# Pre norm's weights on the first token tile by features, and eight identity products ahead of the work

## Chip, cores and metric

The kernel runs on one core of one Trainium2 chip. The metric is the device time of one execution in microseconds; several executions of each kernel are timed and their median is taken. Beside the timed runs there is one profiled execution, whose own time stands beside the span of its trace. TensorE (PE) multiplies matrices, VectorE (DVE) and ScalarE (ACT) work elementwise, GpSimd (POOL) does small scalar steps here, and SyncE (SP) mostly issues DMA transfers.

## The reference, cut to what matters

One decoder layer over 1024 tokens of 1024 features, all float32:

```
h = x * rsqrt(mean(x*x) + 1e-6) * pre_norm_g        # per token; pre_norm_g has one weight per feature
z = h @ w_in                                        # 1024 x 6160
... branch A: gated spatial unit; branch B: gated linear attention ...
y = x + rmsnorm(concat(A, B) @ w_out, post_norm_g)
```

Only the first line and the start of the second are touched by the change.

## The kernel before

The tokens are cut into eight tiles of 128 and the features into eight groups of 128. All matmuls need the feature index on the partitions, so each token tile is normalised with tokens on the partitions and then transposed by TensorE against an identity matrix. A product in nearly full float32 precision is made of three float32r products: every operand is kept as a rounded high part and the remainder as a low part (`split`, lines 106 to 108: ScalarE copies to the rounded type, VectorE subtracts), and `mm3` (lines 110 to 115) issues high x high (L113), high x low (L114) and low x high (L115). The normalised and transposed tokens are the tiles `hTh` and `hTl`, "hT" in the trace.

`load(t)` (lines 246 to 250) fetches token tile t on SP's DMA queue, tile 0 in two halves. `prep(t)` (lines 252 to 276) makes hT of it: ScalarE squares and sums (L259 for tile 0, L263 for the others), GpSimd adds epsilon and raises to the power -0.5 (`rsqrt`, L98 or L100, then L103), VectorE multiplies each half of the tile by this number per token and by the weights, which lie in the tile `gain`, repeated over all 128 partitions (L267), TensorE transposes four groups of 128 features into one PSUM bank (L273), and `split` writes the high and low part of the half (L107, L108).

`block_a` (lines 127 to 147) fetches a block of `w_in` of 512 columns in four granules of two feature groups each. A granule is a raw tile of 512 KB, loaded in two DMAs of 256 KB, and its split into high and low parts ("gr" in the trace). There are three raw buffers. The first block's first two granules (`early=2`) are issued on ScalarE's DMA queue and the other two on SP's. The argument `before` is called ahead of every granule; here it issues the load of token tile 1 ahead of granule 2.

`first_block((t,))` (lines 204 to 207) multiplies token tile t by the eight feature groups of the first block, 24 products into one PSUM bank (`proj_tok`, lines 173 to 181). In the loop of lines 292 to 300 the products of tile t stand between the preparation of the tiles behind it.

The order of an engine's instructions is set when the program is built: a scheduler simulates the program and lets each engine take, of what is ready in its simulation, the instruction that stands first in the source. On the chip every engine then runs its list in that order and waits at an instruction whose operands are not there.

The source order before, around the change (lines 278 to 286):

```
load(0, 2)
gain = pre.tile([P, D], F32, name="gain", bufs=1)
nc.sync.dma_start(gain, row_bc(pre_g, D))
prep(0)
blk = block_a(((C_BV, DV), (C_BG, DV)), lambda k2: load(1) if k2 == 2 else None, fine=True, early=2)
load(2)
```

`row_bc` reads the 4 KB of weights once for each of the 128 partitions, so that this transfer writes 512 KB.

Of the kernel before, what the change touches and what calls it, by code (L numbers as in the profile page):

```python
# [8 lines left out]
F32 = mybir.dt.float32  # L9
F32R = mybir.dt.float32r  # L10
U8 = mybir.dt.uint8
AF = mybir.ActivationFunctionType
ALU = mybir.AluOpType
PSUM = bass.MemoryType.PSUM

P = 128
S = 1024
D = 1024
NT = S // P
KT = D // P  # L20
H = 4
DK = 128
DV = 256
# [5 lines left out]
C_Q, C_K, C_BV, C_BG, C_LR = 3072, 3584, 4096, 5120, 6144  # L29
# [4 lines left out]
def hybrid_layer(  # L34
# [16 lines left out]
    nc = tc.nc  # L51
    x, out = x[0], out[0]
    pre_g, w_in, w_a2, b_a2 = pre_g[0], w_in[0], w_a2[0], b_a2[0]
# [3 lines left out]
    def row_bc(v, n):  # L57
        return v.rearrange("(o n) -> o n", o=1).to_broadcast([P, n])
# [10 lines left out]
    def bank():  # L69
        return psum.tile([P, 512], F32, tag="ps", name="ps")  # L70
# [18 lines left out]
    ident = const.tile([P, P], F32, name="ident")  # L89
    make_identity(nc, ident)  # L90

    LINE = 32
# [3 lines left out]
    def rsqrt(dst, mean, more=None):  # L96
        if more is None:
            nc.gpsimd.tensor_scalar(out=dst, in0=mean, scalar1=EPS, scalar2=None, op0=ALU.add)  # L98
        else:
            nc.gpsimd.tensor_scalar(  # L100
                out=dst, in0=mean, scalar1=EPS, scalar2=more, op0=ALU.add, op1=ALU.add
            )
        nc.gpsimd.tensor_tensor(out=dst, in0=dst, in1=neghalf[:, : dst.shape[-1]], op=ALU.pow)  # L103


    def split(hi, lo, src, eng=None):
        nc.scalar.copy(out=hi, in_=src)  # L107
        return (eng or nc.vector).tensor_tensor(out=lo, in0=src, in1=hi.bitcast(F32), op=ALU.subtract)  # L108
# [10 lines left out]
    def granule(shape):  # L119

        g = wts.tile([P, 2] + shape, F32R, tag="gr", name="gr", bufs=4)
        return g[:, 0], g[:, 1]

    def raw_tile(shape):
        return wts.tile([P] + shape, F32, tag="raw", name="raw", bufs=3)

    def block_a(cols, before=lambda k2: None, fine=False, early=0):

        got = []
        for k2 in range(KT // 2):  # L130
            before(k2)
            raw = raw_tile([2, W])
            c = 0
            for c0, n in cols:
                (nc.scalar if k2 < early else nc.sync).dma_start(
                    raw[:, :, c : c + n],
                    w_in[k2 * 256 : (k2 + 1) * 256, c0 : c0 + n].rearrange("(k p) c -> p k c", p=P),
                )
                c += n
            hi, lo = granule([2, W])  # L140
            if fine:
                for j in range(2):
                    split(hi[:, j], lo[:, j], raw[:, j])
            else:
                split(hi, lo, raw)
            got += [(hi[:, j], lo[:, j]) for j in range(2)]
        return got

    def block_b(cols):
# [15 lines left out]
    hTh, hTl = (  # L165
        [hp.tile([P, 4, S], F32R, tag="q", name="hT", bufs=4) for _ in range(2)] for _ in range(2)
    )
# [36 lines left out]
    def first_block(ts):  # L204
        for t, p in zip(ts, proj_tok(ts, blk)):
            nc.scalar.copy(out=v0[:, t], in_=p[:, 0:DV])
            evac_gate(sg0[:, t], p[:, DV:], bg0)
# [29 lines left out]
    def next_unit(after):  # L237
        if units:
            sums = wout_sums(*units.pop(0))
            with tc.issue_after(after.ins):  # L240
                sums()

    with tc.tile_pool(name="pre", bufs=2) as pre:
        xts = {}

        def load(t, n=1):
            xts[t] = pre.tile([P, D], F32, tag="xt", name="xt", bufs=3)
            for i in range(n):
                c = slice(i * D // n, (i + 1) * D // n)
                nc.sync.dma_start(xts[t][:, c], x[t * P : (t + 1) * P, c])  # L250

        def prep(t):
            xt = xts.pop(t)
            h = pre.tile([P, D], F32, tag="h", name="h", bufs=2)
            ss = pre.tile([P, LINE], F32, tag="ss", name="ss", bufs=3)
            halves = [slice(j * W, (j + 1) * W) for j in range(2)]
            if t == 0:
                for j, c in enumerate(halves):
                    nc.scalar.activation(  # L259
                        out=h[:, c], in_=xt[:, c], func=AF.Square, scale=D ** -0.5, accum_out=ss[:, j : j + 1]  # L260
                    )
            else:
                nc.scalar.activation(out=h, in_=xt, func=AF.Square, scale=D ** -0.5, accum_out=ss[:, 0:1])  # L263
            rstd = ss[:, 0:1]
            rsqrt(rstd, rstd, ss[:, 1:2] if t == 0 else None)
            for j, c in enumerate(halves):
                nc.vector.scalar_tensor_tensor(  # L267
                    out=h[:, c], in0=xt[:, c], scalar=rstd, in1=gain[:, c], op0=ALU.mult, op1=ALU.mult
                )
                pt = bank()  # L270
                for k in range(4):
                    kk = 4 * j + k
                    nc.tensor.transpose(pt[:, k * P : (k + 1) * P], h[:, kk * P : (kk + 1) * P], ident)  # L273
                ts = slice(t * P, (t + 1) * P)
                last = split(hTh[j][:, :, ts], hTl[j][:, :, ts], pt.rearrange("p (k c) -> p k c", k=4))
            return last

        load(0, 2)

        gain = pre.tile([P, D], F32, name="gain", bufs=1)  # L280
        nc.sync.dma_start(gain, row_bc(pre_g, D))
        prep(0)
        blk = block_a(
            ((C_BV, DV), (C_BG, DV)), lambda k2: load(1) if k2 == 2 else None, fine=True, early=2
        )
        load(2)
        bg0 = const.tile([P, DV], F32, tag="bg", name="bg0")
        nc.gpsimd.dma_start(bg0, row_bc(bn_g[0:DV], DV))
        nc.sync.dma_start(
            lr_raw, w_in[:, C_LR : C_LR + RANK].rearrange("(k p) c -> p k c", p=P)  # L290
        )
        for t in range(NT - 2):
            first_block((t,))
            if t + 3 < NT:
                load(t + 3)
            if t == 0:
                prep(1)
            last = prep(t + 2)
            if t >= 1:
                next_unit(last)  # L300
# [3 lines left out]
    with tc.tile_pool(name="gla", bufs=1) as gp:  # L304
# [3 lines left out]
            out=causal, in_=causal, pattern=[[1, P]], base=0, channel_multiplier=-1,  # L308
# [11 lines left out]
        for i in range(4):  # L320
# [4 lines left out]
            out=w2[32:64], in0=w2_raw[32:64], in1=w2[32:64].bitcast(F32), op=ALU.subtract  # L325
# [8 lines left out]
        for r, w in enumerate(w_lr):  # L334
            nc.gpsimd.memset(w.bitcast(F32), 0.0)
            src = lr_raw[:, 4 * r : 4 * r + 4]
            for i in (0, 1, 3):
                nc.scalar.copy(out=w[:, :, 32 * i : 32 * i + RANK], in_=src)
            nc.gpsimd.tensor_tensor(
                out=w[:, :, 64 : 64 + RANK], in0=src, in1=w[:, :, 0:RANK].bitcast(F32), op=ALU.subtract  # L340
# [4 lines left out]
        for hf in range(2):  # L345
            first_block((NT - 2 + hf,))
            pl = bank()
            c = slice(hf * 512, (hf + 1) * 512)
            for k in range(KT):
                for i, part in enumerate(hT(k, c)):  # L350
                    nc.tensor.matmul(
                        pl, w_lr[k // 4][:, k % 4], part,
                        start=(k == 0 and i == 0), stop=(k == KT - 1 and i == 1),
# [3 lines left out]
                out=lrT[96:128, c], in0=pl[96:128], in1=lrT[96:128, c].bitcast(F32), op=ALU.subtract  # L357
# [201 lines left out]
    with tc.tile_pool(name="sgu", bufs=1) as sp_:  # L559
# [38 lines left out]
        def third_sum_h(k):  # L598
# [8 lines left out]
            out=wsr, in_=wsr, pattern=[[0, G], [-1, P]], base=0, channel_multiplier=1,  # L607
# [11 lines left out]
        for i in range(2):  # L619
            if i == 1:  # L620
                blk = block_a(((C_V + 512, 512),))
            for n, t in enumerate(range(NT) if i == 0 else (4, 5, 6, 7, 0, 1, 2, 3)):
# [5 lines left out]
                if (i, n) == (0, 4):  # L628
                    for r in range(2):
                        pt = bank()  # L630
                        for g in range(4):
                            nc.tensor.transpose(pt[:, g * P : (g + 1) * P], wsr[:, 4 * r + g], ident)
                        nc.scalar.copy(
                            out=wsT[:, 4 * r : 4 * r + 4], in_=pt.rearrange("p (g c) -> p g c", g=4)
# [5 lines left out]
                if (i, n) == (1, 2):  # L640
                    ones = wide()[:, 0:P]
                    nc.vector.memset(ones, 1.0)
                    for r in range(2):
                        pt = bank()
                        nc.tensor.matmul(
                            pt, ones, wsT[:, 4 * r : 4 * r + 4].rearrange("p g t -> p (g t)"),
                            start=True, stop=True,
                        )
                        for g in range(4 * r, 4 * r + 4):
                            nc.vector.scalar_tensor_tensor(  # L650
                                out=q[:, g], in0=pt[:, (g % 4) * P : (g % 4 + 1) * P],
                                scalar=gb[:, 1, g : g + 1], in1=q[:, g], op0=ALU.mult, op1=ALU.add,
# [300 lines left out]
```

## Time and profile before

| | us |
|---|---|
| median of 3 runs | 778.92 |
| lowest, highest run | 777.01, 778.99 |
| the profiled execution's own time | 777.7 |
| span of its trace (first to last instruction) | 776.0 |
| TensorE busy in it | 748.8 |

The times in the trace count from the start of the span. "Busy" counts instructions that run, not what an engine waits for; matmuls are pipelined and overlap, so the step from one to the next is shorter than a matmul's duration. Behind a row, square brackets hold the idle time of the engine in front of it and what ended it. The line numbers are those of the kernel printed above.

### The profile page before, as it was taken

The numbers are of one execution on the slowest core, as the hardware profiler recorded it, in microseconds if no ns is written. First come the engines' busy times: TensorE is split into PE (matmuls) and PEld (weight loads), VectorE is DVE, ScalarE is ACT, GpSimd is POOL, SyncE is SP. The second block draws the span as 40 slices with busy tenths as digits, with TensorE's granted clock in tenths as the row PEclk, the third lists the DMA queues.
The fourth block names the chain that finished last, engine by engine and source line by source line (L and its number), as shares of the span: only waits on it lengthen the run. The fifth ranks groups of instructions, "written<-read, shape, count | busy, mean of one in ns | idle before, by whom it ended". The sixth has DMA issues, their size and how long they took to land.

```text
span 776.0 us, 10096 instructions
## 1 busy us (share of the span) xinstructions
PE 748.8 (97%) x3676; PEld 620.9 (80%) x3676; DVE 498.2 (64%) x862; ACT 389.8 (50%) x680; POOL 128.8 (17%) x167
## 2 busy tenths in 40 slices
PE   4999999999999999999999999999999999999996
PEld 3887788787888778888878888888888778888885
DVE  4756599746576575653897388656555497534665
ACT  5546567646273735443442227665665652434431
POOL 2333243512222222322100000000000000000043
PEclk9999999999999999999999999999999999999999
DMA  9636510343712562243220022112112595346157
GB/s 311 214 110 205 162 55 2 109 162 109 224 55 102 167 200 82 82 163 109 82 82 1 0 55 58 53 54 55 55 54 66 189 372 216 109 162 245 55 217 271
DMA packets 79938, 98.39 MB, mean 127 GB/s; under 512 B 5584, under 2 KB 62928, under 8 KB 79888
## 3 DMA queue, kind: packets, MB, share of 16 engines
q1 hardware_dynamic: 76224, 89.21, 34.9%
q0 software_dynamic: 2000, 6.43, 2.7%
q10 hardware_dynamic: 1664, 2.10, 0.8%
q8 instruction: 29, 0.48, 0.2%
q14 instruction: 21, 0.17, 0.1%
HBM read 72.56 MB, written 25.17 MB: 126 GB/s over the span
## 4 chain that ended last, share of the span: by engine, by line
PE 72%; DVE 9%; DMA 7%; ACT 6%; issue 3%; SPq 1%; POOL 1%; DVEq 0%; POOLq 0%; ACTq 0%
PE ps L113 23%; PE ps L115 23%; PE ps L114 23%; DMA wb<-in_w_out_dram 3%; DMA wo_d<-wb 2%; PE ps L672 2%; DMA xt<-in_x_dram 1%; DVE wb L224 1%; DVE wb L108 1%; DVE gr L108 1%; SPq L221 1%; POOL f L394 1%; DMA a<-mix_d 1%; DVE og L490 1%; PE ps L497 1%
## 5 line engine op out<-in xcount | busy, mean ns | idle before, releaser
L113 PE MATMUL ps<-gr,hT 128*128 128x512 f32 x384 | 152.0, 398 | 1.6 <-ACT gr L107 1.1
L115 PE MATMUL ps<-gr,hT 128*128 128x512 f32 x384 | 149.7, 391 | 0.0
L114 PE MATMUL ps<-gr,hT 128*128 128x512 f32 x384 | 149.6, 392 | 0.0
L108 DVE TENSOR_TENSOR gr<-raw,gr 128x1024 fp32r<-128x1024 f32 (+1 forms) x97 | 91.1, 960 | 25.2 <-ACT gr L107 24.4
L113 PE MATMUL ps<-hT,gr 128*128 128x512 f32 x256 | 100.3, 394 | 0.7 <-ACT u L745 0.7
L114 PE MATMUL ps<-hT,gr 128*128 128x512 f32 x256 | 100.0, 391 | 0.0
L115 PE MATMUL ps<-hT,gr 128*128 128x512 f32 x256 | 99.1, 394 | 0.2 <-DVE gr L108 0.2
L107 ACT CAST gr<-raw 128x1024 fp32r<-128x1024 f32 (+1 forms) x97 | 79.0, 837 | 29.6 <-PE ps L115 16.3
L113 PE MATMUL ps<-gr,ah 128*128 128x512 f32 x216 | 84.1, 390 | 2.4 <-ACT ah L107 2.4
L113 PEld LDWEIGHTS ps<-gr,hT 128*128 128x128 f32 x384 | 72.5, 189 | 16.6 <-ACT gr L107 1.5
L115 PEld LDWEIGHTS ps<-gr,hT 128*128 128x128 f32 x384 | 72.4, 189 | 14.7 <-DVE hT L108 0.2
L114 PE MATMUL ps<-gr,ah 128*128 128x512 f32 x216 | 84.0, 389 | 0.0
L114 PEld LDWEIGHTS ps<-gr,hT 128*128 128x128 f32 x384 | 72.5, 189 | 13.7
L115 PE MATMUL ps<-gr,al 128*128 128x512 f32 x216 | 82.9, 389 | 0.0
L224 DVE TENSOR_TENSOR wb<-wb 128x256 f32<-128x256 f32 x64 | 28.7, 448 | 44.4 <-DMA wb<-in_w_out_dram 43.7
L115 PEld LDWEIGHTS ps<-hT,gr 128*128 128x128 f32 x256 | 48.1, 188 | 10.8 <-DVE gr L108 0.9
L113 PEld LDWEIGHTS ps<-hT,gr 128*128 128x128 f32 x256 | 48.1, 188 | 10.3 <-ACT u L745 1.2
L114 PEld LDWEIGHTS ps<-hT,gr 128*128 128x128 f32 x256 | 48.1, 188 | 9.6
L113 PEld LDWEIGHTS ps<-gr,ah 128*128 128x128 f32 x216 | 40.6, 188 | 11.2 <-ACT ah L107 2.8
L107 ACT CAST ah<-a 128x512 fp32r<-128x512 f32 x38 | 23.5, 623 | 49.8 <-PE ps L114 42.7
L114 PEld LDWEIGHTS ps<-gr,ah 128*128 128x128 f32 x216 | 40.6, 188 | 8.4
L115 PEld LDWEIGHTS ps<-gr,al 128*128 128x128 f32 x216 | 40.6, 188 | 8.3
(224 smaller groups left out, 1315.0 us busy)
## 6 DMA issues: line engine op xcount, KB each, us to landing
raw<-in_w_in_dram SPq DMA_DIRECT2D x76, 256.0 KB, 3.2
gr<-wo_d SPq DMA_DIRECT2D x16, 1024.0 KB, 4.8
wb<-in_w_out_dram SPq DMA_DIRECT2D x64, 128.0 KB, 2.6
wo_d<-wh SPq DMA_DIRECT2D x16, 512.0 KB, 2.8
wo_d<-wb SPq DMA_DIRECT2D x16, 512.0 KB, 2.9
raw<-in_w_out_dram SPq DMA_DIRECT2D x12, 512.0 KB, 4.0
mix_d<-mixB POOLq DMA_DIRECT2D x8, 512.0 KB, 3.1
raw<-in_w_in_dram SPq DMA_DIRECT2D x8, 512.0 KB, 3.8
```

The source lines that it names most:

```text
L107: nc.scalar.copy(out=hi, in_=src)
L108: return (eng or nc.vector).tensor_tensor(out=lo, in0=src, in1=hi.bitcast(F32), op=ALU.subtract)
L113: nc.tensor.matmul(ps, a[0], b[0], start=start, stop=False, **how)
L114: nc.tensor.matmul(ps, a[0], b[1], start=False, stop=False, **how)
L115: nc.tensor.matmul(ps, a[1], b[0], start=False, stop=stop, **how)
L221: nc.sync.dma_start(b[:, i], w_out[(row + j) * P : (row + j + 1) * P, c : c + 256])
L224: sub = lambda out, a, c: nc.vector.tensor_tensor(out=out, in0=a, in1=c, op=ALU.subtract)
L394: nc.gpsimd.tensor_tensor(out=f, in0=b[:, :, CH - 1 : CH].to_broadcast([P, 8, CH]), in1=b, op=ALU.subtract)
L490: nc.vector.tensor_scalar_mul(og[:, i], og[:, i], oss[:, i : i + 1])
L497: nc.tensor.transpose(ptv[:, k, i], og[:, i, k * P : (k + 1) * P], ident)
L672: nc.tensor.matmul(pt[:, c], part[:, c], wsT[:, g], start=True, stop=True)
```

## The change

For token tile 0 alone, the weights are no longer multiplied in before the transposition. VectorE multiplies the tile by the number per token only (a tensor by one scalar per partition), TensorE transposes, and the weights come in behind that: features then lie on the partitions, so a weight is one scalar per partition. ScalarE copies each group of 128 features with that scalar as its scale, and VectorE makes the low part in one instruction (product minus the high part). Each of the two engines issues four instructions of 128 columns per half where it issued one of 512.

For this the weights are needed as a column per feature group. They are loaded as 8 rows of 128 on ScalarE's DMA queue (4 KB), transposed by TensorE once and copied by VectorE to `gain_col`. The repeated tile `gain`, which tiles 1 to 7 go on using, is loaded later: ahead of granule 3, behind the loads of token tile 1 and of granule 2 on SP's queue.

In front of `prep(0)` eight products of the identity matrix with itself are issued, into a PSUM bank that nothing reads.

```diff
@@ prep(t) @@
             for j, c in enumerate(halves):
-                nc.vector.scalar_tensor_tensor(
-                    out=h[:, c], in0=xt[:, c], scalar=rstd, in1=gain[:, c], op0=ALU.mult, op1=ALU.mult
-                )
+                if t == 0:
+                    nc.vector.tensor_scalar_mul(h[:, c], xt[:, c], rstd)
+                else:
+                    nc.vector.scalar_tensor_tensor(
+                        out=h[:, c], in0=xt[:, c], scalar=rstd, in1=gain[:, c], op0=ALU.mult, op1=ALU.mult
+                    )
                 pt = bank()
                 for k in range(4):
                     kk = 4 * j + k
                     nc.tensor.transpose(pt[:, k * P : (k + 1) * P], h[:, kk * P : (kk + 1) * P], ident)
-                ts = slice(t * P, (t + 1) * P)
-                last = split(hTh[j][:, :, ts], hTl[j][:, :, ts], pt.rearrange("p (k c) -> p k c", k=4))
+                if t > 0:
+                    last = split(hTh[j][:, :, ts], hTl[j][:, :, ts], pt.rearrange("p (k c) -> p k c", k=4))
+                    continue
+                for k in range(4):
+                    g, src = gain_col[:, 4 * j + k : 4 * j + k + 1], pt[:, k * P : (k + 1) * P]
+                    nc.scalar.activation(out=hTh[j][:, k, ts], in_=src, func=AF.Copy, scale=g)
+                    last = nc.vector.scalar_tensor_tensor(
+                        out=hTl[j][:, k, ts], in0=src, scalar=g, in1=hTh[j][:, k, ts].bitcast(F32),
+                        op0=ALU.mult, op1=ALU.subtract,
+                    )
             return last
 
         load(0, 2)
 
+        g_rows = pre.tile([KT, P], F32, name="g_rows", bufs=1)
+        nc.scalar.dma_start(g_rows, pre_g.rearrange("(k p) -> k p", p=P))
+        gain_col = pre.tile([P, LINE], F32, name="gain_col", bufs=1)
         gain = pre.tile([P, D], F32, name="gain", bufs=1)
-        nc.sync.dma_start(gain, row_bc(pre_g, D))
+        pt = bank()
+        nc.tensor.transpose(pt[:, 0:KT], g_rows, ident[0:KT, 0:KT])
+        nc.vector.tensor_copy(gain_col[:, 0:KT], pt[:, 0:KT])
+
+        idle = bank()
+        for _ in range(8):
+            nc.tensor.matmul(idle[:, 0:P], ident, ident, start=True, stop=True)
         prep(0)
+
+        def more(k2):
+            if k2 == 2:
+                load(1)
+            if k2 == 3:
+                nc.sync.dma_start(gain, row_bc(pre_g, D))
+
         blk = block_a(
-            ((C_BV, DV), (C_BG, DV)), lambda k2: load(1) if k2 == 2 else None, fine=True, early=2
+            ((C_BV, DV), (C_BG, DV)), more, fine=True, early=2
         )
```

## Rows read from the trace of the kernel before

**Rows 1.** The page's busy time, share of the span and instructions of each engine.

```profile
PE 748.8 (97%) x3676; PEld 620.9 (80%) x3676; DVE 498.2 (64%) x862; ACT 389.8 (50%) x680; POOL 128.8 (17%) x167
```

**Rows 2.** Timeline of TensorE, 10 to 21 us: start, duration, engine, line, what.

```profile
10.72 1.97 PE L273 MATMUL ps<-ident,h 128*128 128x128 f32 x8 [10.72 <-DVE h L267]
...
13.21 0.79 PE L113 MATMUL ps<-gr,hT 128*128 128x512 f32 x1 [0.52 <-ACT hT L107]
...
16.36 1.08 PE L273 MATMUL ps<-ident,h 128*128 128x128 f32 x8
...
17.20 0.49 PE L114 MATMUL ps<-gr,hT 128*128 128x512 f32 x1
...
20.07 1.03 PE L273 MATMUL ps<-ident,h 128*128 128x128 f32 x8
```

**Rows 3.** Chain of waits, 0 to 32 us: start, us to the next link, what.

```profile
14.43 0.43 PE ps L115
...
17.68 0.23 PE ps L115
```

**Rows 4.** Timeline of POOL, VectorE (DVE) and ScalarE (ACT), 0 to 16 us.

```profile
2.21 0.31 POOL masks.py:199 TENSOR_SCALAR_AFFINE_SELECT ident<-ident 128x128 f32<-128x128 f32 x1
...
5.56 0.63 ACT L259 ACTIVATE h<-xt 128x512 f32<-128x512 f32 x1 [0.95 <-DMA xt<-in_x_dram]
...
6.77 0.57 POOL L103 TENSOR_TENSOR ss<-ss,neghalf 128x1 f32<-128x1 f32 x1
...
7.00 1.29 DVE L108 TENSOR_TENSOR gr<-raw,gr 128x512 fp32r<-128x512 f32 x2 [6.04 <-ACT gr L107]
...
9.91 1.42 DVE L267 SCALAR_TENSOR_TENSOR h<-xt,ss,gain 128x512 f32<-128x512 f32 x2 [1.62 <-DMA gain<-in_pre_norm_g_dram]
...
11.53 1.06 ACT L263 ACTIVATE h<-xt 128x1024 f32<-128x1024 f32 x1 [4.05 <-DMA xt<-in_x_dram]
...
12.59 0.57 ACT L107 CAST hT<-ps 128x512 fp32r<-128x512 f32 x1
...
13.80 1.41 DVE L267 SCALAR_TENSOR_TENSOR h<-xt,ss,gain 128x512 f32<-128x512 f32 x2
```

**Rows 5.** Same timeline, the queues of SyncE (SPq) and ScalarE (ACTq): DMA issues.

```profile
0.79 1.50 ACTq L135 DMA_DIRECT2D raw<-in_w_in_dram  x3
...
1.71 0.42 SPq L281 DMA_DIRECT2D gain<-in_pre_norm_g_dram  x1
...
3.89 0.37 ACTq L135 DMA_DIRECT2D raw<-in_w_in_dram  x1
...
6.68 0.88 SPq L250 DMA_DIRECT2D xt<-in_x_dram  x1
```

**Rows 6.** DMA issues in windows about 1.71, 3.89, 6.68 us: KB, us to landing.

```profile
gain<-in_pre_norm_g_dram SPq DMA_DIRECT2D x1, 512.0 KB, 8.1
...
raw<-in_w_in_dram ACTq DMA_DIRECT2D x1, 256.0 KB, 8.8
...
xt<-in_x_dram SPq DMA_DIRECT2D x1, 512.0 KB, 7.9
```

**Rows 7.** What the DMA engines moved, 0 to 30 us in 40 slices.

```profile
GB/s 0 0 120 212 238 380 373 320 67 272 393 384 407 376 374 414 414 312 322 371 377 418 423 358 407 365 346 346 343 386 375 284 322 328 369 224 268 399 87 0
```

**Rows 8.** Groups by line, shapes apart: count | busy us, mean ns | idle before.

```profile
L490 DVE TENSOR_SCALAR og<-og,oss 128x256 f32<-128x256 f32 x32 | 13.8, 469 | 2.5 <-POOL oss L103 2.4
...
L206 ACT COPY mixB<-ps 128x256 f32<-128x256 f32 x8 | 3.0, 371 | 12.6 <-PE ps L115 12.6
...
L107 ACT CAST hT<-ps 128x512 fp32r<-128x512 f32 x16 | 8.8, 599 | 0.8 <-PE ps L273 0.8
...
L375 ACT ACTIVATE f<-ps,ba 128x512 f32<-128x512 f32 x8 | 5.5, 690 | 6.8 <-PE ps L438 6.7
...
L650 DVE SCALAR_TENSOR_TENSOR q<-ps,gb,q 128x128 f32<-128x128 f32 x8 | 2.1, 340 | 0.0
```

**Rows 9.** Timeline of TensorE, 456.5 to 459.5 us.

```profile
456.82 1.95 PE L672 MATMUL ps<-wsT,vn 128*128 128x128 f32 x16
```

More of the change, by code (lines that the diff above doesn't have):

```diff
@@ L255, in prep @@
             ss = pre.tile([P, LINE], F32, tag="ss", name="ss", bufs=3)
+            ts = slice(t * P, (t + 1) * P)
             halves = [slice(j * W, (j + 1) * W) for j in range(2)]
```

## The prediction

> **What bounds the kernel now.** I read the page's busy shares first: TensorE is busy 97% of the span [rows 1], so the time follows from when its work begins and how little it stands afterwards. The timeline of TensorE comes next [rows 2]. Nothing runs on it until 10.72 us; then come eight transposes of token tile 0, and at 13.21 the first product of the input projection. The steps are the second thing to see: the chain of waits spaces products by 0.43 us at 14.43 and by 0.23 us at 17.68 [rows 3]. A product has 512 columns, so 0.43 us is the 1.2 GHz level and 0.23 us nearly the 2.4 GHz one. Seven products fit between 13.21 and 16.36 at the lower level, and by 17.20 the upper one is granted. From there the projection runs without a gap.
>
> So the change can win at the start alone: what ends the wait before 13.21? The timeline of the other engines answers [rows 4]. The reciprocal root of tile 0 is there at 7.34 (6.77 + 0.57, POOL). VectorE, free at 8.29, then stands 1.62 us until pre norm's weights have landed, and makes h from 9.91. ScalarE has its own delay: the square of tile 1 stands in front of tile 0's copies in its queue and waits for tile 1's tokens until 11.53, so the first copy begins at 12.59, though the first four transposes were long done. The weights were issued at 1.71 [rows 5] and took 8.1 us to land [rows 6], and the DMA engines move 310 to 420 GB/s without a break from 7.5 to 22 us [rows 7]: the whole first stretch is supplied at the limit of the DMA engines.
>
> **The change, part by part.**
>
> *The small load and the column of weights.* The new row load goes on ScalarE's DMA queue, where an issue costs 0.5 us (1.50 for three) [rows 5]. Everything behind it, table load included, moves by 0.5 us; the second square waits for its tokens until 5.56 anyway [rows 4], which hides it. If that cover is gone, it costs at most 0.5. The transposition of 8 rows and an 8-column copy run while TensorE and VectorE wait. Nothing.
>
> *h without the weights' wait.* VectorE goes on when the root is there. I take 8.3, behind both subtractions for weight granule 0; 7.6 if h is put between them. For its duration the nearest row is a tensor by one scalar per partition, 256 wide, 0.469 us [rows 8]; 256 more elements at about 1 ns make 0.74, as the old form's 1.42 for two. The Trainium skill, VectorE: DVE Perf Modes (The perf-mode tier table), gives such an fp32 operation between SBUF tiles two elements a cycle; worked out from its figures, an estimate, that is 0.42 a half, and h would be 0.3 us sooner. The 0.469 row speaks against it, and the row stays in the sum. TensorE followed h's start by 0.81 (9.91 to 10.72), so the transposes start at 9.1. Eight took 0.84 at the upper level (16.36 to 17.20), so four take about 0.84 at the lower: copies from 10.1 with the hand-over.
>
> *Eight narrow copies and eight narrow subtractions.* The copies of 256 and 512 columns take 0.371 and 0.599 us [rows 8], which makes 0.26 at 128. The pointer operand adds 0.09 (0.690 against 0.599): 0.35, so the first product can start at 10.5. The subtraction with a scalar at 128 columns from PSUM is in the trace: 0.340. VectorE pays 8 x 0.34 against 2 x 0.68, 1.4 us more, covered by the 1.62 it stood. Three products of one k take 1.3 us at the lower level, so neither engine holds TensorE after the first k. Ends for this step: 9.8 with h early; 11.3 if the square of tile 1 stays in front of the copies and its tokens land when the weights did (9.8, then 1.06 from that square's start to the first copy's, 12.59 less 11.53, then 0.35).
>
> *The weights' load moved.* On SP's queue it now goes past tile 1's tokens and both loads of granule 2, and stands ahead of tile 2's tokens, which were issued at 6.68 and took 7.9 us. So it lands near 14.6; with its own 512 KB no longer in front, 13.3. Tile 1's h, which needs it, began at 13.80 [rows 4]: between 0.5 sooner (then its root decides, so 0) and 0.8 later. VectorE's queue behind that h holds subtractions of granules 1 and 2. Tile 2's tokens come a load later, about 1.3 us; its transposes ran only at 20.07 [rows 2], without a wait, and I cost it at nothing; a tile 2 that comes late would cost what lies over that. Granule 1's last part was issued at 3.89 and took 8.8 us [rows 5, 6], landing at 12.7; 512 KB less ahead of it are worth 1.3 us at 390 GB/s, but tile 1's tokens take some of that, so I take 12.0, and 12.6 with the cast.
>
> *The eight products of the identity.* The nearest row is 16 fp32 products of this size in 1.95 us at the upper level [rows 9], so eight take about 2.0 at the lower: from 2.52, when the identity is finished, to 4.5. They stand in no one's way. Their worth to the clock lies between nothing and the whole low stretch. I take nothing: TensorE then stands for over 4 us, and the eight transposes of before, followed by a shorter stand, left the clock low at 13.21. The Trainium skill, TensorE: Matmul & The Clock Gate (The HAM clock gate), says the same in general: the low clock is the resting state, work lifts it, and idleness brings it back. No row here shows what a pause of 4 us does.
>
> *The sum.* From 10.5, the six products of granule 0 at 0.43 end at 13.1, when granule 1 is ready: no stand. The clock rose 3.2 to 4.0 us after the first product of before; by the same run-up it rises at 14.1. So by 17.2: 6, then 2.3 until 14.1, then 3.1 us less 0.84 for tile 1's transposes, which at 0.23 is 9.8: 18 products, where before had 7, with the same transposes. Eleven products at 0.23 are 2.5 us. 18 is also all there is without granule 3 and tile 1's copies, so I take off 0.1 for a late tile 1: 2.4. Behind that TensorE has full work, so the lead is carried to the end. The profiled execution took 777.7 us (span 776.0), so 775.3; the median of the runs shown, 778.92, is 1.2 above it, so **776.5**. With the late start (11.3, the clock up 4.0 later) the lead is 1.6; with the upper clock throughout and tile 1 ready at once, 3.4. The case's own range is 774.5 to 778.4 with the 1 us that runs scatter to either side.
>
> **The rivals.**
>
> *Supply decides.* For it: the unbroken 310 to 420 GB/s [rows 7]. Against it: TensorE never stood after 13.21. If granules 2 and 3 and tile 1 come no sooner than before, TensorE has 18 products at 17.2 and only granule 3's six to add by 20.07, when before had 7 + 12.5. A lead of 4 products is 0.9 us: 778.0. Chance 0.24.
>
> *The clock stays up from the eight products.* For it: they are real work just before the wait. Against it: the long pause. Granule 0's products would end at 11.5, and granule 1 arrive at 12.6: the time won is mostly spent standing, and the cap of 18 products comes about 0.5 us sooner: 776.0. Chance 0.08.
>
> *Tile 1's weights block VectorE.* If h of tile 1 stands ahead of granule 1's subtraction in VectorE's fixed order and the weights land late, TensorE stops at its seventh product. Landing at 17.1 instead of 13.8, h ends at 18.5 and the subtraction at 19.2; before had 16 products by then, so 2.0 us are lost: 780.9. It decides from a landing at 15.1, and each us more costs one. For it: the moved load goes behind 1 MB more and the old one took 8.1 us. Against it: even the later of the two landings worked out above, 14.6, is short of 15.1. Chance 0.12.
>
> **How the numbers follow.** About 0.3% (2.3 us, below 776.6) is what a measurement can tell from no change. The forecast, 0.56, straddles it: its lead of 1.6 to 3.4 puts 0.38 beyond and 0.18 within. The clock rival adds 0.08 to faster, the supply rival 0.24 to same, the blocking is 0.12 slower. Faster 0.46, same 0.42, slower 0.12. The range, 774.6 to 779.4, holds the first three cases and the milder half of the fourth.
>
> **What would show it.** Right: h of tile 0 near 8.3, the first product near 10.5, steps of 0.23 from about 14, no wait for the weights longer than 1 us, and a page that is otherwise the same. Wrong: a first product after 12; VectorE waiting for the weights while granule 1's casts are done; new gaps of TensorE behind the first tiles; steps of 0.23 from the first product on, which would make the clock rival right; or another order of work far from the start, which would move the time for reasons that I don't count.

## The result and the profile after

The change made the kernel slower. The median after is 783.76 us (782.03 to 784.1, 4 runs) against 778.62 for the kernel before (777.01 to 778.99, 4 runs): a ratio of 1.007, with a 95% interval of 1.0053 to 1.0086. The prediction was 776.5, with a range of 774.6 to 779.4. The profiled execution took 782.03 us, its span 780.3; it is 4.3 us over that of before.

The page's busy time of the changed kernel, and its waits of TensorE (in all, times, longest):

```profile
PE 755.9 (97%) x3693; PEld 626.3 (80%) x3693; DVE 501.4 (64%) x869; ACT 391.2 (50%) x686; POOL 125.9 (16%) x167
```

```profile
PE ps L113 <- ACT hT L283: 5.7, 3, 3.6
...
PE ps L277 <- DVE h L269: 0.9, 1, 0.9
```

TensorE's one long wait at the start, up to 10.72 [rows 2], is gone, but its first products now stop three times for ScalarE's narrow copies (L283), 5.7 us in all. The timeline of the first 21 us tells how. Line numbers from here on are each kernel's own, and shift from one to the next: in the changed kernel L269 is tile 0's h, L277 the transposes, L283 the narrow copies, L284 the narrow subtractions, L302 the eight products.

```profile
0.79 0.60 ACTq L293 DMA_DIRECT2D g_rows<-in_pre_norm_g_dram  x1
...
1.42 0.93 ACTq L135 DMA_DIRECT2D raw<-in_w_in_dram  x2
2.17 0.44 SPq L309 DMA_DIRECT2D gain<-in_pre_norm_g_dram  x1
...
2.65 2.86 SPq L135 DMA_DIRECT2D raw<-in_w_in_dram  x2
...
2.78 3.78 PE L302 MATMUL ps<-ident 128*128 128x128 f32 x16
...
6.97 0.88 DVE L269 TENSOR_SCALAR h<-xt,ss 128x512 f32<-128x512 f32 x2 [3.91 <-POOL ss L103]
...
7.51 1.97 PE L277 MATMUL ps<-ident,h 128*128 128x128 f32 x8 [0.95 <-DVE h L269]
...
11.65 1.14 ACT L107 CAST gr<-raw 128x512 fp32r<-128x512 f32 x2 [1.60 <-DMA raw<-in_w_in_dram]
...
12.30 0.69 DVE L108 TENSOR_TENSOR gr<-raw,gr 128x512 fp32r<-128x512 f32 x1 [4.45 <-ACT gr L107]
...
12.70 0.62 ACT L283 ACTIVATE hT<-ps,gain_col 128x128 fp32r<-128x128 f32 x2
12.91 0.74 DVE L271 SCALAR_TENSOR_TENSOR h<-xt,ss,gain 128x512 f32<-128x512 f32 x1
...
13.11 0.79 PE L113 MATMUL ps<-gr,hT 128*128 128x512 f32 x1 [3.63 <-ACT hT L283]
...
14.18 0.74 DVE L271 SCALAR_TENSOR_TENSOR h<-xt,ss,gain 128x512 f32<-128x512 f32 x1
...
14.84 0.60 DVE L284 SCALAR_TENSOR_TENSOR hT<-ps,gain_col,hT 128x128 fp32r<-128x128 f32 x2
...
15.22 0.59 ACT L107 CAST hT<-ps 128x512 fp32r<-128x512 f32 x1 [1.91 <-PE ps L277]
15.70 1.14 ACT L107 CAST gr<-raw 128x512 fp32r<-128x512 f32 x2
...
16.74 0.63 ACT L283 ACTIVATE hT<-ps,gain_col 128x128 fp32r<-128x128 f32 x2
17.16 0.79 PE L113 MATMUL ps<-gr,hT 128*128 128x512 f32 x1 [0.64 <-ACT hT L283]
...
17.64 0.60 DVE L284 SCALAR_TENSOR_TENSOR hT<-ps,gain_col,hT 128x128 fp32r<-128x128 f32 x2
...
19.81 0.64 ACT L283 ACTIVATE hT<-ps,gain_col 128x128 fp32r<-128x128 f32 x2
20.22 0.61 DVE L284 SCALAR_TENSOR_TENSOR hT<-ps,gain_col,hT 128x128 fp32r<-128x128 f32 x2 [0.17 <-ACT hT L283]
20.24 0.80 PE L113 MATMUL ps<-gr,hT 128*128 128x512 f32 x1 [1.40 <-ACT hT L283]
```

Three things are to be seen. First, h of tile 0 is there early, from 6.97 against 9.91 [rows 4], and its transposes are done by 9.5. Second, ScalarE then has nothing to do but the square of tile 1 (8.90 to 9.96): granule 0 has not landed, and its casts, which stand ahead of the copies in ScalarE's list, wait until 11.65. Third, the copies do not run one behind the other. Two of them (one per half) run at 12.70, two at 16.74 and two at 19.81. Between one pair and the next stand two subtractions of VectorE, at 14.84 and 17.64, with casts of granules, the square of tile 2 and tile 1's h in between. TensorE has 3 products out by 17.0 where the kernel before had 7.

Granule 0's two loads, issued from 1.42, were on their way for 9.1 us (the median of the two); those of the kernel before, issued from 0.79, for 4.5 (DMA issues, windows about these times, first the changed kernel, then the one before):

```profile
raw<-in_w_in_dram ACTq DMA_DIRECT2D x2, 256.0 KB, 9.1
```

```profile
raw<-in_w_in_dram ACTq DMA_DIRECT2D x2, 256.0 KB, 4.5
```

One more load has moved. SyncE's queue issues granule 2's loads from 2.65 in the changed kernel, and from 4.91 in the kernel before:

```profile
4.91 1.73 SPq L135 DMA_DIRECT2D raw<-in_w_in_dram  x2
```

The clock comes last. In the chain of waits the steps of one product are still 0.43 us at 23.27 and 0.23 from 24.88; in [rows 3] they were 0.23 at 17.68.

```profile
23.27 0.43 PE ps L114
...
24.88 0.23 PE ps L114
```

The loss is complete after 24 products. The table gives, from TensorE's timelines, the start of some of the 168 products that make up the first part of the projection, and of the last instruction on TensorE: for the kernel before the time, for the others the difference, in us. (The profile of e6 was taken of a disturbed run of 844 us, with a granted clock of 0.85 from about 11 us on, so only its first products are given; its median leaves that run out.)

| kernel | median us (lowest to highest, runs) | 1st | 7th | 24th | 49th | 168th | last |
|---|---|---|---|---|---|---|---|
| before | 778.62 (777.01 to 778.99, 4) | 13.21 | 15.93 | 21.86 | 28.32 | 58.97 | 769.06 |
| after | 783.76 (782.03 to 784.1, 4) | -0.10 | +4.31 | +5.36 | +5.37 | +5.42 | +4.40 |
| e1 two loops | 781.98 (780.24 to 783.4, 4) | -0.94 | +0.55 | +1.78 | +1.85 | +1.93 | +5.80 |
| e2 no products | 780.77 (779.12 to 785.74, 10) | -0.86 | +3.46 | +4.37 | +4.36 | +4.39 | +3.10 |
| e3 gain first | 780.59 (779.25 to 784.3, 6) | +0.03 | +1.01 | +2.63 | +2.69 | +2.75 | +2.98 |
| e4 before, products | 779.18 (777.11 to 781.07, 10) | +0.20 | +0.21 | +1.14 | +1.15 | +1.15 | +1.31 |
| e5 small load on SyncE | 783.58 (783.24 to 785.72, 6) | -0.03 | +2.13 | +1.10 | +1.25 | +1.17 | +8.12 |
| e6 all mended | 778.04 (776.68 to 780.47, 11) | -1.77 | -2.18 | | | | |
| e7 before, pinned | 777.67 (775.43 to 779.5, 12) | -0.92 | -1.27 | +0.04 | +0.06 | +0.06 | +1.40 |
| e8 pinned, turns | 780.42 (778.16 to 785.3, 12) | -1.82 | -0.63 | +1.14 | +1.21 | +1.25 | +3.57 |
| e9 products first | 778.01 (775.9 to 779.77, 12) | -4.13 | -3.83 | -1.62 | -1.52 | -1.58 | -0.62 |
| e10 granule 3 early | 776.44 (774.87 to 778.58, 12) | -4.09 | -4.50 | -3.90 | -2.00 | -1.96 | -2.02 |
| e11 without products | 775.81 (773.28 to 777.16, 12) | -3.63 | -3.37 | -3.36 | -1.50 | -1.46 | -0.47 |
| e12 before, granule 3 | 778.04 (775.15 to 779.55, 12) | -1.06 | -1.06 | -1.01 | +0.09 | +0.09 | +1.87 |

Behind the columns of products stands one profiled execution of each kernel, and single executions scatter by 2 us and more. The column "168th" shows what the change and the edits do at the start, but about 1 us of it can be the clock alone: in e4 the steps fall to 0.23 only after 18.1, in the kernel before by 17.2, and that is most of e4's 1.15 us. The column "last" holds in addition what happens far from the start.

### The profile page after: what moved, and what is told of

Read it like the earlier page. It is cut to its first block, busy times and chain, and to the rows that moved or that the text cites. A ratio compares the mean times of both kernels' runs of the same rounds, so it can differ in the third digit from the quotient of the medians.

```text
span 780.3 us, 10145 instructions
## 1 busy us (share of the span) xinstructions
PE 755.9 (97%) x3693; PEld 626.3 (80%) x3693; DVE 501.4 (64%) x869; ACT 391.2 (50%) x686; POOL 125.9 (16%) x167
## 4 chain that ended last, share of the span: by engine, by line
PE 74%; DVE 9%; DMA 7%; ACT 5%; issue 2%; SPq 1%; POOL 1%; ACTq 0%; DVEq 0%; POOLq 0%
PE ps L113 23%; PE ps L115 23%; PE ps L114 23%; DMA wb<-in_w_out_dram 2%; DMA wo_d<-wb 2%; PE ps L700 2%; DMA raw<-in_w_in_dram 2%; SPq L221 1%; PE ps L379 1%; DVE wb L224 1%; DVE gr L108 1%; DVE wb L108 1%; DVE og L518 1%; DMA a<-mix_d 1%; DVE stl L108 1%
## 5 line engine op out<-in xcount | busy, mean ns | idle before, releaser
L115 PEld LDWEIGHTS ps<-hT,gr 128*128 128x128 f32 x256 | 48.1, 188 | 10.5 <-DVE gr L108 0.5
L113 PEld LDWEIGHTS ps<-gr,ah 128*128 128x128 f32 x216 | 40.6, 188 | 11.2 <-ACT ah L107 2.7
```

Of the source, the lines that this page charges most:

```text
L113: nc.tensor.matmul(ps, a[0], b[0], start=start, stop=False, **how)
L115: nc.tensor.matmul(ps, a[1], b[0], start=False, stop=stop, **how)
```

## The experiments

Theory A: copies and subtractions of one PSUM bank take turns, through two queues full of other work. Theory B: granule 0 is late. Theory C: the eight products and the clock. The kernel before ran beside each group, and the ratios are to these runs: 778.47 us (21 runs) beside e1 to e4, 778.03 (28) beside e5 to e8, 777.72 (35) beside e9 to e12.

### e1: copies in one loop, subtractions in a second

```diff
                 for k in range(4):
                     g, src = gain_col[...], pt[...]
                     nc.scalar.activation(out=hTh[j][:, k, ts], in_=src, func=AF.Copy, scale=g)
+                for k in range(4):
+                    g, src = gain_col[...], pt[...]
                     last = nc.vector.scalar_tensor_tensor(
```

> Edit to the changed kernel: the four copies of a half stand in one loop and the four subtractions in a second one behind it; the work is the same. Theory A (each narrow copy waits for the subtraction in front of it, because both read one PSUM bank, and so eight steps go to and fro between two queues that are full of other work): the copies of tile 0 run back to back, the three waits of TensorE for them, 5.7 us, shrink to the first, 3 to 4 us, the clock rises before 19 us, and the time is 779 to 780.5, 3.3 to 5 us under the changed kernel. Rival B (granule 0 of the weights lands at 11.6 us in place of 5.8 because of the order of the loads): the first product stays at 13.1 and no more than 1.5 us come back: 782.3 or more. Rival C (the eight products and their place): no difference, 783.8.

Measured: 781.98, ratio 1.0055 (1.0033 to 1.0076). ScalarE's timeline:

```profile
10.81 1.14 ACT L107 CAST gr<-raw 128x512 fp32r<-128x512 f32 x2 [0.90 <-DMA raw<-in_w_in_dram]
11.85 2.17 ACT L283 ACTIVATE hT<-ps,gain_col 128x128 fp32r<-128x128 f32 x8
```

The same eight copies now take 2.17 us in one stretch instead of being strewn over 9.3 (12.70 to 22.00), and the loss at the 168th product falls from 5.42 to 1.93. Granule 0 is nearly as late as in the changed kernel (cast at 10.81 instead of 11.65). So with two loops 3.5 of the 5.4 us come back in this pair of executions. The median fell by 1.8 only, less than the 3.3 to 5 that theory A gave, and the intervals of the two ratios overlap; the cleaner measure of the turns is e8 against e6 below. This execution lost 3.9 us more behind the 168th product, of which a wait for vh near 268 us is 1.9 (2.8 here, 0.9 before).

### e2: no products, e4: the products alone

```diff
-        for _ in range(8):
-            nc.tensor.matmul(idle[:, 0:P], ident, ident, start=True, stop=True)
```

> Edit to the changed kernel: the eight products of the identity are left out. Theory A and rival B: they ran from 2.8 to 6.6 us, ahead of anything that TensorE could do, and left the clock at its lower level: 783.8, within 1 us. Rival C (the products cost, or they help): 2 us or more to one side.

> Edit to the kernel before: only the eight products of the identity are put in front of tile 0. Theory A and rival B: they end before the first transposes, the steps of the first products stay at 0.43 us, 778.6 within 1 us. Rival C: 781 or more if they hold something up, 777 or less if they raise the clock.

Measured: e2 780.77, ratio 1.0047 (1.0028 to 1.0066); e4, which adds them to the kernel before, 779.18, ratio 1.0012 (0.9996 to 1.0027). The products don't help in either. Whether they cost something stays open: e2's median is 3.0 us under that of the changed kernel, which by the expectation would be theory C's sign, but at the 168th product only 1.03 of the 5.42 us come back, and the runs (779.12 to 785.74, and 782.03 to 784.1) overlap. Most of the loss is there without them.

### e3: the repeated weights loaded first again

```diff
         gain = pre.tile([P, D], F32, name="gain", bufs=1)
+        nc.sync.dma_start(gain, row_bc(pre_g, D))
...
-            if k2 == 3:
-                nc.sync.dma_start(gain, row_bc(pre_g, D))
```

> Edit to the changed kernel: the load of the repeated weights goes back to its place behind tile 0's tokens. Theory A: the copies of tile 0 still go to and fro with the subtractions, the last one after 19 us, and the time stays at 781.5 to 784. Rival B (order of the loads): granule 0 lands by 8 us, the first product is at 10 to 11 us, and the time is 778 to 779.5.

Measured: 780.59, ratio 1.0049 (1.0025 to 1.0073). ScalarE and TensorE:

```profile
11.78 1.14 ACT L107 CAST gr<-raw 128x512 fp32r<-128x512 f32 x2 [6.51 <-DMA raw<-in_w_in_dram]
...
13.23 0.80 PE L113 MATMUL ps<-gr,hT 128*128 128x512 f32 x1 [5.23 <-ACT hT L283]
```

Granule 0 is late all the same, so the moved load of the repeated weights isn't why. The small load ahead of granule 0 on ScalarE's queue is left, and so are granule 2's loads, issued at 2.66 here too. The time lies between the two forecasts. The loss at the start halves (2.75): the builder dealt another order, with pairs of copies at 14.12 and 14.89 where the changed kernel had them at 16.74 and 19.81.

### e5: the small load on SyncE's queue

```diff
-        nc.scalar.dma_start(g_rows, pre_g.rearrange("(k p) -> k p", p=P))
+        nc.sync.dma_start(g_rows, pre_g.rearrange("(k p) -> k p", p=P))
```

> The changed kernel with one word changed: the small load goes on SyncE's queue, behind tile 0's tokens, and no longer in front of granule 0 on ScalarE's. By theory B (granule 0 is late because the small load stands in front of it) granule 0 is back at about 4.5 us instead of 11.6, and where that lateness was the loss, the first product comes at 9 to 10.5 and the time falls to 777 to 779. By theory A (copies and subtractions of one PSUM bank take turns through two in-order queues full of other work) granule 0 comes back early and it helps little, since the program's fixed order on ScalarE now puts granule 1's and 2's casts and the second square in front of the first copy: first product at 14 or later, its 49th at or past 31, time 780.5 to 784.

Measured: 783.58, ratio 1.0073 (1.0049 to 1.0098). ScalarE, then TensorE:

```profile
6.20 1.14 ACT L107 CAST gr<-raw 128x512 fp32r<-128x512 f32 x2
...
10.61 2.25 ACT L107 CAST gr<-raw 128x512 fp32r<-128x512 f32 x4
12.77 0.62 ACT L283 ACTIVATE hT<-ps,gain_col 128x128 fp32r<-128x128 f32 x2
```

```profile
6.49 3.78 PE L302 MATMUL ps<-ident 128*128 128x128 f32 x16
10.06 1.91 PE L277 MATMUL ps<-ident,h 128*128 128x128 f32 x8
...
64.20 3.78 PE L379 MATMUL ps<-hT,w_lr 128*128 128x512 f32 x8 [3.67 <-POOL w_lr L367]
```

Granule 0 is back (cast at 6.20). The edit sent granule 2's loads back too (4.71 instead of 2.65), so it shows that the small load's place matters, not by which way. The first product comes no sooner: the list on ScalarE has granules 1 and 2 ahead of the copies, as theory A had it. But A's place was wrong: at the 168th product only 1.17 us are lost, not 3 or more, and the rest of the 5.6 us falls behind it, where GpSimd's w_lr came late and TensorE stood 3.67 us. The two edits of e1 and e5 thus each mend a part, 3.5 and 4.25 us of 5.42 at the 168th product, which overlap; neither alone mends the time. A second wait shows that no theory had: the small load now lands at 6.3, and the eight products and tile 0's transposes stand behind its transposition on TensorE, so the transposes start at 10.06 instead of 7.51.

### e6, e7, e8: the order pinned

`behind` opens `tc.issue_after` for tile 0's last copy, its last subtraction and its 18th product; e6 has it with e1's and e5's edits, e8 with e5's alone, e7 on the kernel before.

```diff
+                with behind(k2 >= 1, "copy", "sub"):
                     for j in range(2):
                         split(hi[:, j], lo[:, j], raw[:, j])
...
             if t == 0:
-                prep(1)
+                with behind(True, "copy", "sub", "mm"):
+                    prep(1)
```

> The changed kernel with the small load on SyncE's queue, the copies and the subtractions of a half in two loops, and the order pinned: the casts of granules 1 and on, and tile 1's norm, are issued behind tile 0's copies and subtractions. By theory A with B nothing is left of either cause: eight copies back to back from about 8.2 us, first product at 8.5 to 10.5, products of tile 0 then paced by granule 1 (near 12) as the prediction had it, the 49th product 1 to 4 us earlier than the kernel before, time 776 to 779. By theory C (the change loses because the waits around the first products keep the clock at its lower level) the lower level still stands until about 24 us and the 49th product is no earlier than before, time 780 or more. A later wait near 266 us may add or take 1 to 2 us by either.

> The kernel before with the same pins of order alone: granules 1 and on and tile 1's norm behind tile 0's split. A control: where the order alone gains something without the change, e6 owes it to that. Theory A expects nothing at the first product (13.2, it waits for the weights' load and h), perhaps 0 to 1 us of tile 1's transposes leaving the path of tile 0's products; time 777 to 780.

> e6 with copies and subtractions again in one loop, so that they take turns on a bank, but with nothing else in the two queues between them. If taking turns costs by itself (four rounds of a copy of 0.31, a subtraction of 0.34 and two handovers for each half), the last k is ready some 3 us later than in e6 and the 49th product up to 3 us later. If it cost only because other work stood between the turns, TensorE, which spends 2.6 us on the six products of a granule at the lower clock, is slower than the turns: the 49th product within 1 us of e6's and the time within 1 us of it.

Measured: e6 778.04, ratio 1.0005 (0.999 to 1.002): the loss is gone, where theory C gave 780 or more, but the gain isn't there. Its first product came at 11.44 instead of 8.5 to 10.5, behind the wait for the small load that e5 showed. e7 777.67, ratio 0.9991 (0.9975 to 1.0008): the order alone does nothing that can be told. e8 780.42, ratio 1.0034 (1.0015 to 1.0053), 2.4 us above e6, from which it differs by the turns alone, though nothing else stands between them. Its ScalarE with one row of VectorE, then TensorE:

```profile
10.97 0.37 ACT L296 ACTIVATE hT<-ps,gain_col 128x128 fp32r<-128x128 f32 x1 [3.68 <-PE ps L290]
11.76 0.63 ACT L296 ACTIVATE hT<-ps,gain_col 128x128 fp32r<-128x128 f32 x2 [0.42 <-DVE hT L297]
12.16 0.61 DVE L297 SCALAR_TENSOR_TENSOR hT<-ps,gain_col,hT 128x128 fp32r<-128x128 f32 x2 [0.44 <-ACT hT L296]
12.55 0.62 ACT L296 ACTIVATE hT<-ps,gain_col 128x128 fp32r<-128x128 f32 x2 [0.16 <-DVE hT L297]
13.34 0.62 ACT L296 ACTIVATE hT<-ps,gain_col 128x128 fp32r<-128x128 f32 x2 [0.16 <-DVE hT L297]
14.38 0.37 ACT L296 ACTIVATE hT<-ps,gain_col 128x128 fp32r<-128x128 f32 x1 [0.42 <-DVE hT L297]
14.65 2.17 ACT L109 CAST gr<-raw 128x512 fp32r<-128x512 f32 x4
```

```profile
15.31 0.50 PE L115 MATMUL ps<-gr,hT 128*128 128x512 f32 x1 [2.16 <-ACT gr L109]
```

Here the turns can be read clean: what ends the wait in front of each pair of copies is VectorE's subtraction of the pair before, and a round takes 0.79 us (11.76 to 12.55 to 13.34). The eight copies last 3.8 us instead of 2.17, and granule 1's cast behind them, which TensorE needs at 13.1, comes at 14.65. So taking turns costs by itself too; the expectation that TensorE is slower than the turns left out the cast that waits behind them.

### e9 to e12: the products first, granule 3 early

e9 is e6 with the eight products written ahead of the small transpose. e10 also issues granule 3's loads ahead of tile 2's tokens, the lr weights and w_out's first pieces; e11 is e10 without the products; e12 is e7 with the early granule 3.

```diff
+            if early:
+                pin["raw"] = d
...
+        with behind(True, "raw"):
             load(2)
...
+            with behind(True, "raw"):
                 nc.sync.dma_start(b[:, i], w_out[...])
```

> e6 with the eight products written ahead of the small transpose, so that they no longer stand behind the small load (which landed at 6.1 to 6.3 us in e5, e6 and e8, and held back the products and with them tile 0's transposes to 9.9). Theory A with this new wait: transposes at about 7, first product at 8.2 to 9.5 instead of 11.4. Supply theory (TensorE then waits for granules 1 to 3, whatever it did before): the lead over e6 of 2 to 3 us is given back for the most part as waits for granule casts before 19 us, and w_lr comes at 58 to 60 (59.9 before), time 775.5 to 778.5.

> e9 with granule 3's loads issued ahead of tile 2's tokens, the lr weights and w_out's first pieces on SyncE's queue (at about 8 us instead of 11.7). Supply theory: the wait for granule 3 goes, w_lr 1 to 3 us earlier than in e9, time 774 to 777, faster than the kernel before if the later wait near 266 us takes nothing back. If supply isn't what holds it (the wait is for casts behind the copies on ScalarE), as e9 within 0.5 us.

> e10 without the eight products. What the products are worth once nothing else holds the start: if they raise the clock before the transposes, e10 has its first 24 products at 0.23 us each and this one most of them at 0.43, so this one is 1 to 3 us later at w_lr unless it waits for granules anyway. If granules decide (supply), within 0.7 us of e10 and the products are worth nothing.

> e7 (the kernel before, order pinned) with the same earlier loads of granule 3: the control for e10 without any of the change. e7 waited 0.95 us for granule 3; with it earlier, w_lr 0.5 to 1 us earlier than e7's, time 776 to 777.5. If e10 beats this one by 1 us or more, the early transposed weights are worth something of their own; if not, all of e10's gain is the order of the loads.

Measured: e9 778.01, ratio 0.9999 (0.9985 to 1.0014); e10 776.44, ratio 0.9982 (0.9969 to 0.9995); e11 775.81, ratio 0.9969 (0.9954 to 0.9983); e12 778.04, ratio 0.9994 (0.998 to 1.0008). TensorE in e10, then in e11:

```profile
8.00 1.10 PE L293 MATMUL ps<-ident,h 128*128 128x128 f32 x8 [1.43 <-DVE h L285]
9.12 0.50 PE L115 MATMUL ps<-gr,hT 128*128 128x512 f32 x1
...
12.68 0.50 PE L116 MATMUL ps<-gr,hT 128*128 128x512 f32 x1 [0.75 <-DVE gr L110]
...
18.84 1.38 PE L293 MATMUL ps<-ident,h 128*128 128x128 f32 x8 [0.48 <-DVE h L287]
```

```profile
7.96 1.97 PE L293 MATMUL ps<-ident,h 128*128 128x128 f32 x8 [1.46 <-DVE h L285]
9.58 0.78 PE L115 MATMUL ps<-gr,hT 128*128 128x512 f32 x1
```

With the new waits ahead of it taken away, the first product starts at 9.1, four us before that of the kernel before. What becomes of such a lead e9 shows: -4.13 at the first product, -1.62 at the 24th, and nothing in the time. Its chain of waits between 8 and 21 us goes back to one transfer, tile 2's tokens:

```profile
6.12 8.13 DMA xt<-in_x_dram
...
14.27 1.16 ACT h L277 x2
...
17.86 0.67 PE ps L290 x4
```

They land at 14.25, hardly sooner than before (6.68 and 7.9 make 14.6 [rows 5, 6]), and the transposes of tile 2 stand in TensorE's list ahead of every product behind the 18th. In e10 granule 3 overtakes them. Its lead of 3.90 at the 24th product is in part a matter of counting, as tile 2's transposes now follow that product, but two us reach the 168th, 0.4 more than in e9. The medians of the two lie 1.6 apart; the rest of that falls behind the start and stays open. The same loads on the pinned kernel before (e12) shorten its wait for a granule from 0.95 us (e7) to 0.27 and yet give nothing, not the 776 to 777.5 that was expected: in e12 the steps stay at 0.43 until 16.15, in e7 until 14.15. What weights by features are worth is read from e11 against e12, which differ in nothing else than the weights and their loads: 1.55 us at the 168th product, 2.2 in the medians (for e10, with the products, 2.05 and 1.6).

The eight products show no gain even here. They had the clock up for the transposes (1.10 us for eight in e10, 1.97 in e11), and e11 is 0.5 us later at the 168th product, yet its median is lower by 0.6, with runs that overlap. e11 is faster than both kernels, than the one before by 0.31% (0.17 to 0.46).

## Why the prediction was wrong

*The step that failed: "Eight narrow copies and eight narrow subtractions".* Its durations were right: 0.35 was taken for a copy and 0.340 for a subtraction, and single ones took 0.37 and 0.34 to 0.35. What failed is "neither engine holds TensorE after the first k". It summed each engine by itself, as if ScalarE could copy k + 1 while VectorE subtracts k. Both read the same PSUM bank, and the rows of e8 show the next copy waiting for the subtraction, at 0.79 a round. The Trainium skill, PSUM — Partial Sum Buffer (Terms), says why a program must order them so: two engines on one bank and one quarter of the partitions at the same time are an error there, reads against reads included. The rows agree as far as the order goes: in e8 a copy at 12.55 waits for the subtraction of its own half (12.16 to 12.51) and starts while that of the other half, in another bank, still runs (until 12.77). No run shows the error itself. That the two share an SBUF tile, which the copies write and the subtractions read, isn't the reason: the two casts of granule 0 also write one tile, read from SBUF, and in the changed kernel the second doesn't wait for the subtraction of the first part, which starts only at 12.30, when the second cast already runs (two in 1.14 us from 11.65). In `split` taking turns costs one hand-over for 512 columns; the change made four of it, and in the changed kernel every hand-over also waits its turn behind casts, squares and tile 1's h in two ordered queues. e1, which has one hand-over a half, is 3.5 us better at the 168th product; e6 against e8 puts the turns alone at 2.4 us of the time.

*"The small load and the column of weights", costed at nothing.* I named the second square as the cover and asked what stands behind the small load on ScalarE, not what stands behind it on ScalarE's DMA queue: granule 0. Its casts went from 6.2 (e5) to 11.65. This is the second cause, though what delays granule 0 is open: wherever it was late (the changed kernel, e1, e2, e3), granule 2's loads were also issued 2 us sooner, at 2.65. It sets 13.11 as the first product where 10.5 was forecast. Moving the load made another wait (e5), as its transposition is first in TensorE's list.

*"h without the weights' wait".* Right in the main, and better than forecast: h at 6.97 instead of 8.3. Part of that is luck: VectorE was free because granule 0 was late. Where it wasn't (e9, e10), h stood between granule 0's two subtractions, at 7.42 and 7.46, near the 7.6 that the prediction gave for that place. It took 0.44 us a half, where I had put 0.74. Here the Trainium skill was right against my row: VectorE: DVE Perf Modes (The perf-mode tier table) led to an estimate of 0.42, and the 256-wide row of 0.469 [rows 8] misled me; why that one takes as long for half the width isn't shown.

*"The weights' load moved".* Wrong in its place: the program's list on SP had it at 2.17, ahead of granule 2, not behind it. I went by the source, and it is the builder that deals the order. It isn't what made granule 0 late (e3).

*"The eight products".* No gain shows, as taken. They took 3.78 us, not 2.0: a float32 product is two records of the trace (x16 for the eight), so the sixteen of [rows 9] were eight products. So TensorE stood 0.95 us behind them, not over 4. They were too long to hide where the small load came late (e5, e6, e8).

*"The sum".* 18 products by 17.2 was the forecast; there were 4 started. The upper level of the clock, put at 14.1, came at about 24.5, after TensorE had stood three times (3.63, 0.64 and 1.40 us). The late start, 9.8 + 1.06 + 0.35, is 11.2, not 11.3. A lead of 2.4 us was worked out, and with the waits mended and granule 3 early 1.96 is left at the 168th product in e10. That the two are near is in part luck: e10 starts 1.4 us sooner than forecast and gives back two of its four us.

*The rivals.* Supply decides (0.24) is in part what e9 shows once the new waits are gone: a lead of 4.13 shrinks to 1.62 by the 24th product for want of tile 2's tokens. That e9's time, 778.01, is the 778.0 of that rival is luck: 1.58 us of lead are left at the 168th product, as much as in e11 (1.46), whose median is 2.2 lower; e9 loses them behind the start, and why is open. Tile 1's weights block VectorE (0.12, 780.9) came nearest in time, and its place was half right: tile 1's h (12.91 and 14.18) does stand ahead of tile 0's first subtraction at 14.84. But it wasn't the weights that were late; the order was. The clock rival fell in the changed kernel, where the transposes took 1.97 us; in e10 the clock did stay up. No rival had an engine of the pair wait for the other.

## What to carry to other kernels

Before one wide operation is cut into narrow ones for two engines, count the hand-overs between them, not only the durations: here the two readers of one PSUM bank took turns, and each turn waited behind whatever else stood in both queues; with all of one engine's pieces first that went away (e1, e6). Price a load that is put at the head of a queue by what lands behind it as well. And ask of a lead which transfer ends it: in e9 4.13 us shrank to 1.62, as tile 2's tokens came no sooner.

## What the runs showed of the hardware

A 4 KB load, issued in 0.6 us ahead of two loads of 256 KB on one queue, went with a landing 9.1 us after their issue instead of 4.5. With the load on the other queue (e5) the casts began at 6.20 again, and e3 rules out the moved load of the repeated weights. It isn't settled whether the small load does it itself or by way of granule 2's loads, which the other queue issued at 2.65 with it there and at 4.5 to 4.9 without; no run parts the two.

In e5 a long wait was paid twice. TensorE stood 3.67 us for w_lr, and the granted clock was at half behind it (windows of TensorE and the other engines, PE busy first, PEclk third from the right):

```profile
60.00:64.00 4.00, 0.52 (x3) 0.10 (x1) 2.40 (x5) 1.66 (x9) 4.00 (x8) 0.93 0.62 200
64.00:68.00 4.00, 3.80 (x9) 3.03 (x10) 2.82 (x7) 0.00 (x0) 3.34 (x8) 0.50 0.38 119
```

The eight products behind it took 3.78 us, against 2.13 in the kernel before.

The eight identity products, from 2.6 or 2.8 us on, had the clock up at tile 0's transposes in e1, e3, e9 and e10 (1.09 to 1.10 us for eight), and not in the changed kernel (1.97). TensorE stood 0.95 us in between there, and 0.66 to 1.65 in the four. In e9 the level fell again at the first products (steps of 0.43 from 9.55 to 12.11), in e10 it didn't. What decides is open. Open too is what moves the time behind the 168th product: the wait for vh near 266 us varied from 0.75 (e11) to 2.8 (e1) from kernel to kernel, and runs of one kernel lie 2 to 7 us apart.
